# A two-layer block with a mixture of experts: the experts' feed-forward in 4 slabs of 896 columns instead of 7 of 512, and their outputs kept in DRAM

## The chip, the cores and the metric

The kernel runs on one core of one Trainium2 chip. The metric is the device time of one execution in microseconds; the kernel before was timed in three runs. TensorE is written PE, VectorE DVE, ScalarE ACT, GpSimd POOL, and SP is SyncE, which issues the loads of the weights.

## The reference

The input is 256 tokens of 1024 numbers with 16 learned meta tokens ahead of them, all in float32. Each of two layers has a mixer (a pooled branch and differential attention, gated and projected) and a feed-forward. The feed-forward of layer 0 is dense, that of layer 1 is a mixture of 8 experts of which every token uses 2.

```python
def moe_swiglu(h, router, wg, wu, wd):
    logits = jnp.einsum('bld,de->ble', h, router).astype(jnp.float32)
    top_vals, top_idx = lax.top_k(logits, TOP_K)
    top_w = jax.nn.softmax(top_vals, axis=-1)
    combine = jnp.sum(jax.nn.one_hot(top_idx, N_EXPERTS, dtype=jnp.float32) * top_w[..., None], axis=-2)
    out = jnp.zeros_like(h)
    for e in range(N_EXPERTS):
        out = out + combine[..., e:e + 1] * swiglu(h, wg[e], wu[e], wd[e])
    return out
```

`swiglu(h, wg, wu, wd)` is `(silu(h @ wg) * (h @ wu)) @ wd`; `wg` and `wu` are 1024 x 3584 per expert, `wd` is 3584 x 1024. The sum with the residual goes through a last RMS norm.

## The kernel before

**Products in parts.** Every float32 operand is split into a rounded part (float32r, "hi") and the rest ("lo"), and a product is three matmuls: hi with hi, hi with lo, lo with hi. The `Weights` class streams all weights in the order in which they are used. SP loads blocks of 1 MB into raw slots (L87); a block is split in two pieces of 128 x 1024, ACT writing `whi` (L97) and DVE `wlo` (L98) into 5 buffers each. A raw slot comes free, and the next load is issued, behind the second split of its block. `take` keeps four pieces split ahead of the products.

**The stage of the mixture.** Layer 0 and the mixer of layer 1 come first. `MoeNorm` then puts the residual into token order (transposes L800, copy to `h2`), the router's logits are formed (L791), DVE finds the two best experts of a token (L821 to L826), and PE forms each token's rank in its expert (L829, L831, `ppos`). `prepare` builds, for an expert, a 0/1 matrix `s` of tokens and 128 slots (L906), gathers its tokens by matmuls of 128 columns into `pgat` (L916), multiplies them with the norm's gain (L920), splits them into `exh` and `exl` (L921, L922), transposes `s` into `sT` (L926) and forms the slots' scales (L928).

An expert has 7 steps of 512 feed-forward columns. In a step `up` runs twice (gate and up): 24 matmuls of 512 columns (L943 to L945) into one PSUM bank, tokens as the stationary operand. SiLU (ACT, L1047) and the product with up (DVE, L1052) give `gs`; `turn` transposes it by 4 PE transposes (L951) and splits it into `hh` and `hl`. `down` adds the step before into `y`, two banks of 512 columns, 24 matmuls (L991 to L995):

```python
for hf in range(2):
    nc.tensor.matmul(E.y[hf], h[0][:, f], wh[:, 0, d], start=a, stop=False)
    nc.tensor.matmul(E.y[hf], h[1][:, f], wh[:, 0, d], start=False, stop=False)
for hf in range(2):
    nc.tensor.matmul(E.y[hf], h[0][:, f], wl[:, 0, d], start=False, stop=z)
```

At an expert's end `weigh` scales `y` by the expert's weight and splits it (L1003, L1004), and `scatter` (L1010) brings it to token order with 8 matmuls of 512 columns, which accumulate over all experts in four banks `acc`. After the last expert `down_last` finishes one bank of `y` at a time, DVE adds `h2` and `acc` (L1103), and the last norm runs (L1118).

The order on each engine is that of a list scheduler over the program; `high_priority` and `issue_after` move single pieces.

## Time and profile before

| | us |
|---|---|
| runs | 1619.3, 1621.45, 1621.15 (median 1621.15) |
| span of the profiled execution, first to last instruction | 1617.4 |
| time of the profiled execution itself | not listed beside its span |
| PE / DVE / ACT / POOL busy | 1597.8 / 1334.4 / 1093.7 / 4.8 |
| weights loaded by SP's queue | 449.97 MB, 78.7% of 16 engines' span |

The median stands 3.75 us above the profiled span. Times inside the execution are counted from the span's start. The mixture's first up product starts at 611.16 us, its last down product ends where the last scatter starts, at 1603.80. Starts of matmuls that follow each other are compared, not their listed durations, since they overlap on PE.

### The profile page before, as it was taken

How to read it: one execution, taken by the hardware profiler on the slowest of the kernel's cores; microseconds unless marked ns; L12 is line 12 of the kernel's file. 1: busy time of each engine (PE TensorE's matmuls, PEld its weight loads, DVE VectorE, ACT ScalarE, POOL GpSimd, SP SyncE). 2: the span in 40 equal slices, each digit the busy share in tenths (PEclk: the TensorE clock that was granted, in tenths of full speed). 3: DMA queues.
4: the chain of work that ended last, by engine and by line, in shares of the span. 5: the costliest groups of instructions: out<-in, count | busy, mean ns of one | idle time of the engine just before them, and what ended most of it. 6: DMA issues, size and time to landing. Idle time of an engine off the chain costs nothing. (4 is left out here: it accounts for less than half of the span.)

```text
span 1617.4 us, 24251 instructions
## 1 busy us (share of the span) xinstructions
PE 1597.8 (99%) x9315; PEld 1407.3 (87%) x9315; DVE 1334.4 (83%) x1708; ACT 1093.7 (68%) x1349; POOL 4.8 (0%) x12
## 2 busy tenths in 40 slices
PE   8999999999999999999999999999999999999997
PEld 7989999999999998888888888888888888888885
DVE  7857776666877668998899889998999899899897
ACT  5456554444555657777787787778778778778785
POOL 1000000000000000000000000000000000000000
PEclk9999999999999999999999999999999999999998
DMA  9734555555554588999999999999999999999951
GB/s 307 245 113 150 182 172 169 182 173 168 184 160 142 168 331 312 342 364 360 333 365 357 345 358 358 341 362 361 345 354 364 344 349 374 336 346 377 351 205 41
DMA packets 238897, 452.53 MB, mean 280 GB/s; under 512 B 9386, under 2 KB 82264, under 8 KB 238776
## 3 DMA queue, kind: packets, MB, share of 16 engines
q1 hardware_dynamic: 237264, 449.97, 78.7%
q8 instruction: 75, 1.23, 0.3%
q0 software_dynamic: 384, 0.85, 0.2%
q14 instruction: 46, 0.38, 0.1%
q10 hardware_dynamic: 1128, 0.11, 0.1%
HBM read 449.82 MB, written 1.08 MB: 279 GB/s over the span
## 5 line engine op out<-in xcount | busy, mean ns | idle before, releaser
L97 ACT ACTIVATE whi<-raw 128x1024 fp32r<-128x1024 f32 x852 | 892.5, 1060 | 434.9 <-PE ps L386 200.4
L98 DVE TENSOR_TENSOR wlo<-raw,whi 128x1024 fp32r<-128x1024 f32 x852 | 1020.4, 1223 | 153.6 <-ACT whi L97 132.9
L943 PE MATMUL pup<-whi,exh 128*128 128x512 f32 x896 | 354.1, 395 | 0.1
L944 PE MATMUL pup<-wlo,exh 128*128 128x512 f32 x896 | 351.3, 392 | 0.0
L945 PE MATMUL pup<-whi,exl 128*128 128x512 f32 x896 | 349.9, 390 | 0.0
L945 PEld LDWEIGHTS pup<-whi,exl 128*128 128x128 f32 x896 | 168.2, 188 | 34.9
L943 PEld LDWEIGHTS pup<-whi,exh 128*128 128x128 f32 x896 | 168.3, 188 | 33.8 <-DVE exl L922 0.2
L944 PEld LDWEIGHTS pup<-wlo,exh 128*128 128x128 f32 x896 | 168.5, 188 | 33.3
L991 PE MATMUL y<-whi,hh 128*128 128x512 f32 x440 | 175.0, 398 | 0.0
L992 PE MATMUL y<-whi,hl 128*128 128x512 f32 x440 | 174.0, 396 | 0.0
L995 PE MATMUL y<-wlo,hh 128*128 128x512 f32 x440 | 137.7, 394 | 0.0
L386 PE MATMUL ps<-xh,whi 128*128 128x272 f32 (+1 forms) x448 | 131.9, 300 | 0.4 <-ACT hT L707 0.3
L386 PE MATMUL ps<-xh,wlo 128*128 128x272 f32 (+1 forms) x448 | 126.0, 287 | 0.0
L386 PE MATMUL ps<-xl,whi 128*128 128x272 f32 (+1 forms) x448 | 125.9, 286 | 0.0
L386 PE MATMUL ps<-fh,wlo 128*128 128x272 f32 x432 | 124.9, 289 | 0.0
L386 PE MATMUL ps<-fh,whi 128*128 128x272 f32 x432 | 124.8, 290 | 0.0
L386 PE MATMUL ps<-fl,whi 128*128 128x272 f32 x432 | 124.3, 288 | 0.0
L995 PEld LDWEIGHTS y<-wlo,hh 128*128 128x128 f32 x440 | 82.8, 188 | 19.4
L992 PEld LDWEIGHTS y<-whi,hl 128*128 128x128 f32 x440 | 83.0, 189 | 19.1
L991 PEld LDWEIGHTS y<-whi,hh 128*128 128x128 f32 x440 | 82.9, 188 | 18.3
L386 PEld LDWEIGHTS ps<-xh,whi 128*128 128x128 f32 x448 | 84.5, 191 | 4.4 <-PE s L448 1.1
L386 PEld LDWEIGHTS ps<-xl,whi 128*128 128x128 f32 x448 | 83.5, 188 | 0.3
(287 smaller groups left out, 2024.6 us busy)
## 6 DMA issues: line engine op xcount, KB each, us to landing
raw<-in_moe_w_gate_dram SPq DMA_DIRECT2D x112, 1024.0 KB, 5.5
raw<-in_moe_w_up_dram SPq DMA_DIRECT2D x110, 1024.0 KB, 5.7
raw<-in_moe_w_down_dram SPq DMA_DIRECT2D x108, 1024.0 KB, 5.8
raw<-in_w_in_dram SPq DMA_DIRECT2D x30, 1024.0 KB, 6.3
raw<-in_dense_w_gate_dram SPq DMA_DIRECT2D x14, 1024.0 KB, 5.1
raw<-in_dense_w_up_dram SPq DMA_DIRECT2D x14, 1024.0 KB, 5.1
raw<-in_dense_w_down_dram SPq DMA_DIRECT2D x14, 1024.0 KB, 5.0
raw<-in_w_out_dram SPq DMA_DIRECT2D x8, 1024.0 KB, 5.1
```

The costliest lines, as they stand in the source:

```text
L97: self.nc.scalar.activation(hi, w, AF.Copy)
L98: self.nc.vector.tensor_sub(lo, w, hi.bitcast(F32))
L386: newest[0] = nc.tensor.matmul(ps, w_[part][:, k, ms_], xp[:, k, sl], start=t == 0 and k == 0, stop=t == 2 and k == nk - 1).ins
L943: nc.tensor.matmul(ps, E.xh[:, k], wh[:, i], start=k == 0, stop=False)
L944: nc.tensor.matmul(ps, E.xh[:, k], wl[:, i], start=False, stop=False)
L945: nc.tensor.matmul(ps, E.xl[:, k], wh[:, i], start=False, stop=k == NCH - 1)
L991: nc.tensor.matmul(E.y[hf], h[0][:, f], wh[:, 0, d], start=a, stop=False)
L992: nc.tensor.matmul(E.y[hf], h[1][:, f], wh[:, 0, d], start=False, stop=False)
L995: nc.tensor.matmul(E.y[hf], h[0][:, f], wl[:, 0, d], start=False, stop=z)
```

## The change

Everything about layer 0 and the mixer of layer 1 keeps its products. In the mixture:

- **Slabs.** An expert has 4 slabs of 896 columns (`SLAB`), each computed as two halves of 448 columns in two PSUM banks (`SW`). A slab takes 2 x 96 matmuls of 448 columns (L1006), 7 transposes (L1018) and 42 matmuls of 512 columns for `y` (L1044). In the mixture that is 3072 up matmuls of 448 columns in place of 2688 of 512, the same 1344 of `y`, the same 224 transposes in 32 turns in place of 56.
- **Order in a product.** `up` alternates between the two banks in the pattern that `y` has: two matmuls on one bank, two on the other, and for the lo part of the weights one and one.
- **Whole blocks.** A mixture block is 128 x 1792 (gate, up) or 128 x 2048 (down; the last of a slab 128 x 1024), is loaded as one DMA and split by one ACT and one DVE instruction (L115, L116) into 4 hi and 3 lo buffers. Raw slots in the mixture are 13 in place of 16. A row in DRAM is 3.5 KB (896 columns) for gate and up; the block of down takes two neighbouring rows (8 KB) to a partition, so that the columns of `gs` go to the transposes with a stride of 2 (`chunk`).
- **Gain.** The residual is multiplied with the norm's gain on DVE in token order (`h2g`, L843), and `prepare` does not multiply `pgat`.
- **Outputs in DRAM.** `h2` is written to `hdram` (POOL's queue). `keep` scales an expert's `y` on ACT into `yout` and POOL's queue writes it to `ydram`; `weigh` and `scatter` stay for the last expert only, and `sT` is made for it only. In the last expert's slabs 1 and 2, `residual` loads the residual back (`hsum`), gathers each token's rows from `ydram` by four indirect DMAs, and adds them on DVE. Row numbers are formed in `overflow_data`, which also clears one row of `yout` (L950).

```diff
+    def slot(self, i, name):
+        return self.slots[i].tile([P, 2048], F32R, tag=f"w{i}", name=name)
...
+        if large:
+            m = self.n_large
+            self.n_large += 1
+            parts = [self.slot(m % NHI, f"whi{b}"), self.slot(NHI + m % NLO, f"wlo{b}")]
...
+    def add_down(e, s, c0, m):
+        for b in range((NSC + 1) // 2):
+            r = s * SLAB + b * 256
+            n = min(2, NSC - 2 * b)
+            src = moe_w_down[0, e, r:r + n * P, c0:c0 + m]
+            blocks.append((src.rearrange("(p k) f -> p k f", k=n), 1, None))
...
-                nc.scalar.activation(self.h2[:, t, hf * 512:hf * 512 + 512], pt, AF.Copy)
+                d = slice(hf * 512, hf * 512 + 512)
+                nc.vector.tensor_mul(self.h2g[:, t, d], pt, self.gain[:, d])
+                nc.scalar.activation(self.h2[:, t, d], pt, AF.Copy)
                 nc.scalar.activation(pt, pt, AF.Square, accum_out=self.sq[:, t, hf:hf + 1])
+            if hf:
+                nc.gpsimd.dma_start(hdram.rearrange("(t p) d -> p t d", p=P), self.h2)
...
+    def up(E, name, between=None):
+        ps = two(name)
+        for b in range(4):
...
+            wh, wl = ws.take()
+            for w, xs_ in ((wh, (E.xh, E.xl)), (wl, (E.xh,))):
+                for i in range(2):
+                    k = b * 2 + i
+                    for hf in range(2):
+                        f = slice(hf * SW, (hf + 1) * SW)
+                        for x_ in xs_:
+                            nc.tensor.matmul(ps[:, hf, 0:SW], x_[:, k], w[:, i, f], start=k == 0 and x_ is E.xh and w is wh,
+                                             stop=k == NCH - 1 and w is wl)
+        return ps[:, :, 0:SW]
+
+    def chunk(ci):
+
+        b, i = ci // 2, ci % 2
+        return slice(b * 256 + i, (b + 1) * 256, 2) if ci < NSC - 1 else slice(b * 256, SLAB)
+
+    def turn(hs, hh=None, hl=None):
+        pt = two("pth").rearrange("p h (c s) -> p (h c) s", s=P)[:, 0:NSC]
+        for ci in range(NSC):
+            p = nc.tensor.transpose(pt[:, ci], hs[:, chunk(ci)], ident)
...
+    def keep(E, e):
+        nc.scalar.activation(yout, E.y.rearrange("p h d -> p (h d)"), AF.Copy, scale=E.rc[:, 1:2])
+        nc.gpsimd.dma_start(ydram[e * CAP:(e + 1) * CAP], yout)
...
+    def residual():
+
+        pool, tag = ws.kept.pop(0)
+        hsum = pool.tile([P, 2, D], F32, name="hsum", tag=tag)
+        nc.gpsimd.dma_start(hsum, hdram.rearrange("(t p) d -> p t d", p=P))
+        yield hsum
+        spare_row = exl[:, NE % 2].rearrange("p c s -> p (c s)").bitcast(F32)
+        for t in range(2):
+            for k, to in enumerate((yout, spare_row)):
+                nc.gpsimd.indirect_dma_start(out=to, out_offset=None, in_=ydram[:, :],
+                                             in_offset=bass.IndirectOffsetOnAxis(ap=rows_of[:, t, k:k + 1], axis=0),
+                                             bounds_check=None, oob_is_err=True)
+                nc.vector.tensor_add(hsum[:, t], hsum[:, t], to)
+            yield
```

PE, the up product in the steady part of the mixture. `pup` and `pgate` are the PSUM results, `exh` and `exl` the two parts of an expert's tokens, `whi` and `wlo` those of a piece of weights. Before, all on one bank:

```order
L943 MATMUL pup<-whi_1_9410,exh 128x512
L944 MATMUL pup<-wlo_1_9411,exh 128x512
L945 MATMUL pup<-whi_1_9410,exl 128x512
L943 MATMUL pup<-whi_1_9410,exh 128x512
L944 MATMUL pup<-wlo_1_9411,exh 128x512
L945 MATMUL pup<-whi_1_9410,exl 128x512
```

In the changed kernel, behind the end of one slab (`gs` is the product of gate and up, `pth` its transpose):

```order
L1006 MATMUL pup<-wlo_7112,exh 128x448 x4
L1018 MATMUL pth<-cst,gs 128x128 x7
L1006 MATMUL pgate<-whi_7129,exh 128x448
L1006 MATMUL pgate<-whi_7129,exl 128x448
L1006 MATMUL pgate<-whi_7129,exh 128x448
L1006 MATMUL pgate<-whi_7129,exl 128x448
L1006 MATMUL pgate<-whi_7129,exh 128x448
```

The moving rows went from 512 to 448 columns; hi and lo tokens alternate, each pair on one bank, and the lo weights take four matmuls in a row over both banks.

PE, where an expert's output used to be scattered (`acc` are the four banks in token order, `sT` the transposed slot matrix; the `exh` and `exl` that stand in these rows hold the two parts of the weighted output). Before:

```order
L945 MATMUL pup<-whi_1_9410,exl 128x512
L1010 MATMUL acc_7114<-exh,sT 128x512
L1010 MATMUL acc_7116<-exh,sT 128x512
L1010 MATMUL acc_7115<-exh,sT 128x512
L1010 MATMUL acc_7117<-exh,sT 128x512
L1010 MATMUL acc_7114<-exl,sT 128x512
L1010 MATMUL acc_7116<-exl,sT 128x512
L1010 MATMUL acc_7115<-exl,sT 128x512
L1010 MATMUL acc_7117<-exl,sT 128x512
L943 MATMUL pup<-whi_0_9436,exh 128x512
```

In the changed kernel, the end of an expert's down product and of its turn:

```order
L1018 MATMUL pth<-cst,gs 128x128 x3
L1044 MATMUL y<-wlo_8037,hh 128x512 x4
L1044 MATMUL y<-whi_8054,hh 128x512
L1044 MATMUL y<-whi_8054,hl 128x512
L1044 MATMUL y<-whi_8054,hh 128x512
L1044 MATMUL y<-whi_8054,hl 128x512
L1044 MATMUL y<-wlo_8055,hh 128x512 x2
L1018 MATMUL pth<-cst,gs 128x128 x4
L1006 MATMUL pgate<-whi_8072,exh 128x448
L1006 MATMUL pgate<-whi_8072,exl 128x448
L1006 MATMUL pgate<-whi_8072,exh 128x448
```

No scatter stands there; the transposes are placed inside and behind the down product, and the next gate product follows.

DVE, the router's chain at the end of layer 1's mixer (`m` and `i` the best values and their places, `oh` the one-hot experts, `sel` the chosen ones, `pos` the ranks, `s` the slot matrix). Before:

```order
L821 MAX m_7066<-lg_6785 128x8
L821 MAX m_7066<-lg_6786 128x8
L822 MAX_INDEX i_7067<-m_7066,lg_6785 128x8
L822 MAX_INDEX i_7067<-m_7066,lg_6786 128x8
L869 TENSOR_TENSOR wt<-m_7066 128x2
L823 CAST if_7068<-i_7067 128x4
L824 TENSOR_TENSOR oh<-cst,if_7068 128x32
L826 TENSOR_TENSOR sel<-oh 128x16
L889 COPY pack<-sel 128x16
L833 COPY pos<-ppos 128x16
L866 TENSOR_TENSOR rv<-sq_6787 128x2
L906 TENSOR_SCALAR s<-cst,pos,sel 128x128 x2
```

In the changed kernel (`h2g` the residual times gain, `yout` the row that is cleared):

```order
L866 MAX m_6868<-lg_6609 128x8
L866 MAX m_6868<-lg_6610 128x8
L843 TENSOR_TENSOR h2g<-pth_6885,gainb 128x512
L843 TENSOR_TENSOR h2g<-pth_6893,gainb 128x512
L867 MAX_INDEX i_6869<-m_6868,lg_6609 128x8
L867 MAX_INDEX i_6869<-m_6868,lg_6610 128x8
L918 TENSOR_TENSOR wt<-m_6868 128x2
L950 MEMSET yout 1x1024
L868 CAST if_6870<-i_6869 128x4
L869 TENSOR_TENSOR oh<-cst,if_6870 128x32
L915 TENSOR_TENSOR rv<-sq_6611 128x2
L871 TENSOR_TENSOR sel<-oh 128x16
```

Two multiplications of 512 columns and the clearing of the row of 1024 now stand between MAX and `sel`, and the split ahead of MAX is one of 1792 columns in place of 1024.

## Rows read from the trace of the kernel before

**Rows 1.** The page of the profile, busy time of the engines.

```profile
span 1617.4 us, 24251 instructions
PE 1597.8 (99%) x9315; PEld 1407.3 (87%) x9315; DVE 1334.4 (83%) x1708; ACT 1093.7 (68%) x1349; POOL 4.8 (0%) x12
```

**Rows 2.** Windows of stages: us, busy time of each engine, clock, DMA share, GB/s.

```profile
604.00:608.00 4.00, 3.41 (x17) 3.44 (x18) 2.57 (x19) 2.97 (x4) 0.00 (x0) 0.60 1.03 388
640.00:1560.00 920.00, 920.00 (x4254) 759.95 (x4253) 829.63 (x785) 720.71 (x760) 0.00 (x0) 1.00 0.98 354
```

**Rows 3.** Waits of the queue that issues the loads, 700 to 1500 us: total, times, longest.

```profile
SPq L87 <- DVE wlo L98: 666.2, 264, 4.0
```

**Rows 4.** PE timeline: start, duration, instruction; one up product, one bank.

```profile
1567.13 0.39 PE L943 MATMUL pup<-whi,exh 128*128 128x512 f32 x1
...
1575.06 0.40 PE L945 MATMUL pup<-whi,exl 128*128 128x512 f32 x1
```

**Rows 5.** PE timeline: a y product into two banks, then a turn.

```profile
1575.30 0.40 PE L991 MATMUL y<-whi,hh 128*128 128x512 f32 x1
...
1580.18 0.40 PE L992 MATMUL y<-whi,hl 128*128 128x512 f32 x1
1580.41 0.60 PE L951 MATMUL pth<-cst,gs 128*128 128x128 f32 x4
1580.77 0.48 PE L943 MATMUL pup<-whi,exh 128*128 128x512 f32 x1
```

**Rows 6.** PE timeline: the last y product, one bank, to the last scatter.

```profile
1599.70 0.39 PE L1018 MATMUL y<-whi,exh 128*128 128x512 f32 x1
...
1603.80 0.63 PE L1010 MATMUL acc<-exh,sT 128*128 128x512 f32 x2
```

**Rows 7.** PE timeline: products of 256 columns in layer 1.

```profile
593.49 0.28 PE L386 MATMUL ps<-ml,whi 128*128 128x256 f32 x1
...
596.09 0.28 PE L386 MATMUL ps<-mh,wlo 128*128 128x256 f32 x1
```

**Rows 8.** PE timeline: the scatter of one expert.

```profile
1000.74 1.09 PE L1010 MATMUL acc<-exh,sT 128*128 128x512 f32 x4
...
1002.60 0.39 PE L943 MATMUL pup<-whi,exh 128*128 128x512 f32 x1
```

**Rows 9.** PE timeline: a piece of a gather, and the slots' transposes and scales.

```profile
649.41 0.83 PE L916 MATMUL pgat<-s,h 128*128 128x128 f32 x6
650.00 0.48 PE L944 MATMUL pup<-wlo,exh 128*128 128x512 f32 x1
650.31 0.40 PE L945 MATMUL pup<-whi,exl 128*128 128x512 f32 x1
...
686.91 0.38 PE L926 MATMUL pst<-cst,s 128*128 128x128 f32 x2
687.13 0.51 PE L928 MATMUL pst<-rc,s 128*128 128x2 f32 x4
687.49 0.48 PE L944 MATMUL pup<-wlo,exh 128*128 128x512 f32 x1
```

**Rows 10.** PE timeline: router, first gather and the first up product.

```profile
603.14 0.40 PE L829 MATMUL ppos<-sel,cst 128*128 128x16 f32 x2 [1.36 <-DVE sel L826]
604.59 1.01 PE L916 MATMUL pgat<-s,h 128*128 128x128 f32 x4 [0.83 <-DVE s L906]
...
611.16 0.50 PE L943 MATMUL pup<-whi,exh 128*128 128x512 f32 x1
```

**Rows 11.** Groups of instructions, 700 to 1500 us: busy us, mean ns, idle before.

```profile
L98 DVE TENSOR_TENSOR wlo<-raw,whi 128x1024 fp32r<-128x1024 f32 x541 | 644.9, 1223 | 75.5 <-ACT whi L97 62.6
L955 DVE TENSOR_TENSOR hl<-pth,hh 128x512 fp32r<-128x512 f32 x45 | 30.8, 684 | 0.0
L1052 DVE SCALAR_TENSOR_TENSOR gs<-pup,rcs,gs 128x512 f32<-128x512 f32 x45 | 33.6, 746 | 0.0
```

**Rows 12.** A window in which 1 MB blocks stood queued: same columns as Rows 2.

```profile
576.00:584.00 8.00, 8.00 (x71) 8.00 (x70) 3.86 (x8) 2.63 (x4) 0.00 (x0) 1.00 1.04 400
```

More of the change, by code (lines that the diff above doesn't have):

```diff
@@ L101, in split @@
         if i == npc - 1:
-            self.free.append(self.raw.pop(b)[1])
+            slot = self.raw.pop(b)[1]
+            if self.keep:
+                self.keep -= 1
+                self.kept.append(slot)
+            else:
+                self.free.append(slot)
             self.load()
@@ L107, in take @@
         self.taken += 1
-        while self.n_split < min(q + 1 + self.ahead, len(self.order)):
+        large = self.blocks[self.order[q][0]][2] is None
+        ahead = NLO if large else NPAIR
+        while self.n_split < min(q + ahead, len(self.order)):
+            b = self.order[self.n_split][0]
+            if not large and self.blocks[b][2] is None:
+                break
             self.split()
@@ L910, in prepare @@
         E.yparts = []
+        pg_ = two("pgat").rearrange("p h (c s) -> p (h c) s", s=CAP)
         for hf in range(2):
-            pg_ = bank("pgat")
-            for i in range(4):
-                c = hf * 4 + i
+            for c in range(hf * 4, hf * 4 + 4):
                 for t in range(2):
-                    nc.tensor.matmul(pg_[:, i * P:(i + 1) * P], h2[:, t, c * P:(c + 1) * P], E.s[:, t],
-                                     start=t == 0, stop=t == 1)
-            xh_, xl_ = E.xh[:, hf * 4:hf * 4 + 4], E.xl[:, hf * 4:hf * 4 + 4]
@@ L1069, in tile_block, with between @@
-            prev = (E, j, hs)
+                    next(gen)
+                elif s == 2:
+                    for _ in gen:
+                        pass
+            elif s == 1:
+                fin = residual()
+                hsum = next(fin)
+            elif s == 2:
+                for _ in fin:
+                    pass
+            if end:
+                spare_h = [x_[:, NE % 2, 0:NSC] for x_ in (exh, exl)]
+                def between():
+                    with tc.high_priority():
+                        h, ins = turn(gs, *spare_h)
+                    last_h.append(h)
+                    return ins
+                last_h = []
+                down(prev[0], prev[1], turned, between)
+            else:
+                if prev is not None:
+                    down(prev[0], prev[1], turned)
+                    if prev[1] == NS - 1:
+                        keep(prev[0], e - 1)
+                turned, _ = turn(gs)
@@ L1070, in tile_block @@
+            prev = (E, s)
         if e + 1 < NE:
-            for _ in gen:
-                pass
             E = nE
-    free = [slot for slot in ws.free if slot[0] is mn.raw]
+    free = list(ws.free)
     def spare(shape, name):
```

282 lines of the change are left out of this document (137 added, 145 removed).

## Prediction

> **What bounds the kernel now.** Start at the page: PE is busy 1597.8 of the span of 1617.4 us, DVE 1334.4, ACT 1093.7 [rows 1]. Such a share is an average, so the windows come next: from 640 to 1560 us, nearly the whole mixture, PE is busy 920.00 of 920.00 us at the full granted clock, DVE 829.63 and ACT 720.71 [rows 2]. No wait ends on PE there. The DMA share of 0.98 looks like a second bound, and the queue's waits tell that it isn't: SP waited 264 times, 666.2 us in all, for DVE's splits to free a raw slot, so the loads run ahead and stop for room [rows 3]. The mixture is therefore a dense stream of matmuls, and its time is the number of steps times the time from one start to the next. The change is to be costed on PE's timeline.
>
> **The steps.** Sums are made against the profiled span; the median of the runs is 3.75 us above it, and I carry that over. An up product on one bank goes from 1567.13 to 1575.06 in 35 steps, 0.2266 us each [rows 4]. A y product, which changes banks, goes from 1575.30 to 1580.18 in 21 steps, 0.2324 each [rows 5]. The last y product, on one bank with hi and lo in y's order, takes 18 steps in 4.10 us, 0.2278 [rows 6]. The scatter, which changes banks at every step, takes 8 in 1.86, 0.2325 [rows 8]. So a change of bank goes with about 0.005 us more per step of 512 columns. A step of 256 columns takes 2.60/22 = 0.1182 [rows 7]; from there to 0.2266 is 0.423 ns a column, so that 64 columns are worth 0.0271 us.
>
> The mixture's stream lasts from 611.16 [rows 10] to 1603.80 [rows 6], 992.6 us. In it 2688 up steps by 0.2266 are 609.1, 1344 y steps by 0.2324 are 312.3, seven scatters 13.0, 56 turns by 0.36 (1580.41 to 1580.77 [rows 5]) 20.2. That leaves 38.0. Seven gathers of 32 rows, at 0.59 for 6 [rows 9], are 22.0, and seven pieces of slot work by 0.58 [rows 9] are 4.1. The last 11.9 us are longer steps behind interruptions: the first wide step behind a piece of narrow matmuls takes 0.31 [rows 9] in place of 0.23. There are 91 such interruptions (56 turns, 28 gather pieces, 7 of slot work), so 0.13 each.
>
> **Part by part.**
> - *Slabs.* 3072 steps of 448 columns replace 2688 of 512. The changed up has y's pattern of banks and of hi and lo, so I take y's step less 64 columns: 0.2324 - 0.0271 = 0.2053 us. Bounds: 0.1995 if the premium of bank changes vanishes (0.2266 - 0.0271), 0.2054 if all of the scatter's stays. 3072 x 0.2053 = 630.7 against 609.1: **+21.6** (lower end +3.8). The y steps stay 1344 in their old pattern: 0.
> - *Scatter.* Seven of eight go, all on PE's path: **-13.0**. Their transposes of `s` go too, 686.91 to 687.13 [rows 9], 7 x 0.22 = **-1.5**.
> - *Turns.* The 224 transposes stay, in 32 turns. The changed order cuts the wide stream 71 times in place of 91: 20 x 0.13 = **-2.6**. Their stationary reads now have a stride of 2; no row shows such a read. From below, 0; from above, a doubled transpose, 0.09 more for 192 of them, 17 us. I take 0, since a transpose's weights load beside the work of the step ahead and 0.36/4 is well under a wide step.
> - *Router.* PE waited 1.36 us for `sel` and 0.83 for `s` [rows 10], while the granted clock was 0.60 from 604 to 608 [rows 2], a mean of its levels of 1.2 and 2.4 GHz. DVE's order now has between MAX and `sel` two multiplications of 512 columns (0.68 each by `hl`'s row [rows 11]) and the clearing of 1024 elements of one row (an estimate of 0.9, by the slope below): about +2.4, and the first gather behind it. What comes back: no multiplication of `pgat` between gather and split (0.7, once exposed). I take **+2.0**, between 0 and +5.
> - *Splits.* DVE's row for 1024 columns is 1223 ns, for 512 it is 684 [rows 11]: 1.05 ns a column. A split of 1792 is then 2.03 us, of 2048 2.30. A slab has 8 of the first, 3 of the second and one of 1024, 24.4 us; `hl` and `gs` of 896 columns add 1.1 and 1.15. DVE has 26.7 us of work in a slab of 96 x 0.2053 + 42 x 0.2324 + 0.75 = 30.2: hidden, as ACT's lighter load is. If this cover went, each 1% more on DVE's 26.7 beyond 30.2 would show in full.
> - *DRAM traffic.* `keep`, the residual out and back and the gathers add 0.52 x 7 + 1.05 + 1.05 + 2.1 = 7.8 MB to 352 MB of the mixture's weights (8 x 3 x 1024 x 3584 numbers of 4 bytes): 2%. On 354 GB/s [rows 2] that asks for some 362; with blocks queued the engines moved 400 [rows 12]. Hidden. `keep` holds `y`'s banks for one ACT pass of 1024 columns while the next expert's gate and up run for 20 us: hidden. POOL's queue carries all of the new transfers but has none of the weights behind it. The four adds wait for their gathers, and DVE's splits stand behind them; by the changed order they come a slab after the issue. Bounds 0 to 4 x 2; I take 0.
> - *Tail.* The last y product, one scatter, the last norm: unchanged, 0.
>
> Sum: 21.6 - 13.0 - 1.5 - 2.6 + 2.0 = **+6.5**. 1617.4 + 6.5 + 3.75 = **1627.7 us**, 0.4% slower. With the transition's bounds and 0.001 us either way on 3072 steps the case runs from 1620 to 1634. About 0.2%, or 3.2 us, can be told from no change here.
>
> **Rival 1, not slower: narrower steps carry no premium.** If the extra of bank changes hides under the shorter step, up costs 3072 x 0.1995 = 612.9, 17.8 less, and the time is 1609.9. For it: no row shows two banks at under 512 columns. Against it: y and scatter agree on 0.232 with different patterns. It decides from a step of 0.2021 on, where the sum is 9.8 lower and the result under 1618. The Trainium skill, "TensorE: Matmul & The Clock Gate", section "Wait — 56ns, not 53.3ns?", has a rule of this sort: a step is columns over 2.4 GHz plus about 2.5 ns whatever the matmul does, 189 ns here and 216 for 512 columns, so that up would grow by an estimated 1.0 us only and the time be near 1607. The trace disagrees on 512 columns, with 226.6 and 232.4 ns.
>
> **Rival 2: strided transposes.** If their reads double a transpose, +17 gives 1645. It decides from 0.02 us each (3.8 us). For it: nothing shown. Against it: the load of weights overlaps.
>
> **Rival 3: splits become the bound.** If DVE's wide splits cost 16% more than the line through two points, DVE has 24.4 x 1.16 + 2.25 = 30.55 us per slab, and 0.35 over PE's 30.2 in each of 32 slabs gives +11, 1639; it decides from 14% on, and each further 1% costs 8 us. For it: DVE is already at 0.90 of the stage, and there are 3 lo buffers for 5. Against: each buffer is larger, and a split has 2.46 us of PE work to hide under.
>
> **Chances.** Forecast 0.57, rival 1 0.26, rival 2 0.06, rival 3 0.11. The forecast's case falls to slower with 0.38, to the same 0.16, to faster 0.03; rival 1 gives faster 0.24 and same 0.02; the others are slower. Faster 0.27, same 0.18, slower 0.55. The range goes from 1609 (rival 1 in full) to 1638, which leaves out the far ends of rivals 2 and 3 and little of rival 1.
>
> **What to look for.** In the changed profile: starts of up's matmuls 0.205 us apart (0.1995 is rival 1); no scatter until the end; the step from one transpose to the next 0.09 as now; no waits of PE for `wlo` in the mixture; the first up product at 613. PE waiting for splits, or for weights still under way, would make the prediction wrong; so would a stream that starts 5 us late.

## The result and the profile after

The changed kernel takes 1647.89 us (median of 4 runs, 1647.37 to 1649.53) against 1620.22 for the kernel before on the same chip: ratio 1.0169, 95% interval 1.0155 to 1.0184. The forecast was 1627.7 with a range to 1638: the sign was right, the size was not, and the time lies outside the range. Against +6.5 us the profiled span grew by 28.4, from 1617.4 to 1645.8 (the medians by 27.7). The page's first lines answer to [rows 1]:

```profile
span 1645.8 us, 24255 instructions
PE 1607.7 (98%) x9629; PEld 1471.7 (89%) x9629; DVE 1285.4 (78%) x1356; ACT 1017.9 (62%) x996; POOL 15.9 (1%) x27
```

DVE and ACT are less busy than before, by 49 and 76 us; the span is longer all the same. So no engine took over as the bound by its load. The windows (columns as in [rows 2]) tell where the time went. First of the changed kernel, then the two halves of the mixture in the kernel before:

```profile
604.00:608.00 4.00, 0.95 (x4) 0.86 (x4) 2.64 (x15) 3.95 (x9) 1.22 (x2) 0.83 0.86 310
608.00:612.00 4.00, 2.95 (x14) 2.98 (x15) 3.59 (x26) 1.25 (x2) 0.00 (x0) 0.50 0.54 196
640.00:1100.00 460.00, 460.00 (x2285) 410.83 (x2284) 389.20 (x222) 330.14 (x213) 1.61 (x3) 1.00 0.96 353
1100.00:1560.00 460.00, 453.97 (x2213) 397.89 (x2213) 376.29 (x214) 311.50 (x209) 4.84 (x7) 1.00 0.94 354
```

```profile
640.00:1100.00 460.00, 460.00 (x2137) 380.35 (x2136) 414.81 (x395) 359.56 (x380) 0.00 (x0) 1.00 0.98 354
1100.00:1560.00 460.00, 460.00 (x2119) 379.60 (x2118) 414.82 (x391) 361.15 (x381) 0.00 (x0) 1.00 0.98 355
```

Read the counts of PE beside its busy time. Before, the second half has 18 matmuls fewer than the first; after, 72 fewer. These 54 at 460/2285 us each are 10.9 us, while the window shows only 6.0 of idleness, since part of every standstill counts as busy. A step's listed time is 0.36 us where the next one starts 0.20 later, so that the first 0.16 of a wait lies inside the step ahead of it: in the stream the 25 wide steps ahead of a listed wait are longer than their neighbours by 0.16, the 27 behind one by 0.11, and ten steps from 1586 to 1590 us, behind the longest wait, run at a granted clock of 0.57. These are 8.5 us. In the first half PE never stands still. The loss begins in mid-mixture, in a program whose loop does the same in every slab. The waits of PE from 616 to 1612 us name the engines (total, times, longest); the kernel before had no wait of PE at all from 612 to 1600 us:

```profile
PE pgate L1006 <- ACT whi L115: 2.7, 2, 2.6
PE pup L1006 <- ACT whi L115: 2.6, 10, 0.3
PE y L1044 <- DVE wlo L116: 2.3, 3, 0.8
PE pup L1006 <- DVE wlo L116: 1.7, 10, 0.2
PE pth L1018 <- DVE gs L1120: 1.2, 1, 1.2
```

The splits come late, on engines that are busy for 0.7 and 0.83 of the stage. Are the loads late? No: the queue still waits for free slots, 664.0 us in all from 700 to 1500 us against 666.2 before [rows 3]:

```profile
SPq L94 <- DVE wlo L116: 664.0, 303, 6.7
```

ACT's own waits, from 616 to 1612 us, tell what stands in the way:

```profile
ACT hh L1022 <- PE y L1044: 62.8, 13, 9.2
ACT gs L1118 <- PE pgate L1006: 54.0, 19, 5.4
```

Two more of ACT's instructions wait for PE, `exh` (29.7 us, 8 times) and `yout` (17.0, 4 times); no run moved them. DVE's product with up (`gs`) waits as well:

```profile
DVE gs L1120 <- PE pup L1006: 22.0, 9, 3.8
```

Before, ACT's SiLU waited 16.0 us in 54 waits and never over 0.3, and its copy of the turned slots (`hh`) not at all:

```profile
ACT gs L1047 <- PE pup L945: 16.0, 54, 0.3
```

ACT's timeline of the changed kernel shows one slab early and one late in the mixture:

```profile
712.00 1.71 ACT L115 ACTIVATE whi<-raw 128x1792 fp32r<-128x1792 f32 x1 [0.78 <-PE pgate L1006]
713.61 0.99 ACT L1118 ACTIVATE gs<-pgate,rcs 128x896 f32<-128x896 f32 x1
714.50 1.90 ACT L115 ACTIVATE whi<-raw 128x2048 fp32r<-128x2048 f32 x1
...
1203.06 4.87 ACT L115 ACTIVATE whi<-raw 128x1792 fp32r<-128x1792 f32 x3
1211.98 1.01 ACT L1118 ACTIVATE gs<-pgate,rcs 128x896 f32<-128x896 f32 x1 [4.04 <-PE pgate L1006]
1212.88 10.28 ACT L115 ACTIVATE whi<-raw 128x1792 fp32r<-128x1792 f32 x6
```

At 713 us the SiLU follows splits that already stand ahead of PE. At 1212 ACT has nothing to do for 4.04 us: the SiLU is next in its order and waits for the gate product to end, with six splits behind it, which then run without a pause. PE comes to the end of what is split 2.65 us later:

```profile
1214.63 0.47 PE L1006 MATMUL pup<-whi,exh 128*128 128x448 f32 x1 [0.25 <-ACT whi L115]
```

The instruction order of ACT, which is fixed before anything runs, already has this. The first piece is from the third slab, the second from the twentieth; of its three splits ahead of the SiLU two are still the gate product's own:

```
452 L115 ACTIVATE whi_7465<-raw_7201 128x1792
453 L115 ACTIVATE whi_7483<-raw_7219 128x1792
454 L115 ACTIVATE whi_7504<-raw_7237 128x1792
455 L115 ACTIVATE whi_7522<-raw_7258 128x1792
456 L1118 ACTIVATE gs<-pgate,rcs 128x896
...
696 L115 ACTIVATE whi_11413<-raw_11160 128x1792
697 L115 ACTIVATE whi_11431<-raw_11185 128x1792
698 L115 ACTIVATE whi_11449<-raw_11203 128x1792
699 L1118 ACTIVATE gs<-pgate,rcs 128x896
700 L115 ACTIVATE whi_11467<-raw_11221 128x1792
```

Counted through the program, by blocks split ahead of a SiLU beyond those that its own gate has used, it is 4 in the first 13 slabs and then 3, 3, 2, 1, 2, 2, 1, 1 and so on to the end; ahead of `hh` it falls from 4 to 2. Ahead of DVE's product with up it is 2 blocks in the first 15 slabs and then 1 or 0. In the kernel before it is 4 pieces (once 5) and 5 in all 56 steps. That is the first theory to test: **order**, not load. Its rivals are the price of the steps (448 columns, two banks, the stride), the larger blocks, too few buffers, and the DRAM outputs.

The rest of the 28.4 us stands at both ends. Times by landmark of PE (last transpose of layer 1; first of the steady wide stream; first step of the last y product; end of the span):

| us | before | after | diff |
|---|---|---|---|
| to the last transpose of layer 1 | 601.4 | 602.5 | +1.1 |
| transition | 9.8 | 13.6 | +3.8 |
| the stream | 987.1 | 1002.2 | +15.1 |
| last y product to the end | 19.1 | 27.5 | +8.4 |

Transition, PE's timeline (answers to [rows 10]), then DVE's:

```profile
602.48 0.42 PE L841 MATMUL pth<-cst,hT 128*128 128x128 f32 x2
606.56 0.54 PE L874 MATMUL ppos<-sel,cst 128*128 128x16 f32 x2 [3.67 <-DVE sel L871]
609.05 3.75 PE L975 MATMUL pgat<-s,h2g 128*128 128x128 f32 x16 [1.53 <-DVE s L966]
613.55 0.47 PE L1006 MATMUL pgate<-whi,exh 128*128 128x448 f32 x1 [0.75 <-ACT exh L977]
```

```profile
603.09 0.24 DVE L866 MAX8 m<-lg 128x8 f32<-128x8 f32 x2
603.24 1.27 DVE L843 TENSOR_TENSOR h2g<-pth,gainb 128x512 f32<-128x512 f32 x2
605.01 0.91 DVE L950 MEMSET yout<- 1x1024 f32 x1 [0.15 <-issue]
606.34 0.17 DVE L871 TENSOR_TENSOR sel<-oh 128x16 f32<-128x16 f32 x1
```

`h2g` and the clearing of a row stand between the maximum and `sel`, 1.27 and 0.91 us. PE stands still for 3.67 in place of 1.36, and the clock is at its lower level, 1.2 GHz, from 608 to 612.

### The profile page after: what moved, and what is told of

Same layout as the page of the kernel before. It is cut to its first block, busy times and chain, and to the rows that moved or that the text cites. A ratio compares the mean times of both kernels' runs of the same rounds, so it can differ in the third digit from the quotient of the medians.

```text
span 1645.8 us, 24255 instructions
## 1 busy us (share of the span) xinstructions
PE 1607.7 (98%) x9629; PEld 1471.7 (89%) x9629; DVE 1285.4 (78%) x1356; ACT 1017.9 (62%) x996; POOL 15.9 (1%) x27
## 3 DMA queue, kind: packets, MB, share of 16 engines
q0 software_dynamic: 2688, 9.24, 1.5%
## 5 line engine op out<-in xcount | busy, mean ns | idle before, releaser
L116 DVE TENSOR_TENSOR wlo<-raw,whi 128x1792 fp32r<-128x1792 f32 (+2 forms) x388 | 762.6, 2001 | 130.1 <-ACT whi L115 56.0
L115 ACT ACTIVATE whi<-raw 128x1792 fp32r<-128x1792 f32 (+2 forms) x388 | 637.5, 1682 | 143.1 <-PE y L1044 72.8
L115 ACT ACTIVATE w<-raw 128x1024 fp32r<-128x1024 f32 x180 | 189.7, 1058 | 251.3 <-PE ps L418 185.5
L116 DVE TENSOR_TENSOR w<-raw,w 128x1024 fp32r<-128x1024 f32 x180 | 219.3, 1222 | 66.6 <-ACT w L115 66.1
L1006 PE MATMUL pgate<-whi,exh 128*128 128x448 f32 x512 | 189.1, 369 | 3.5 <-ACT whi L115 2.7
L1006 PE MATMUL pup<-whi,exh 128*128 128x448 f32 x512 | 188.2, 368 | 2.6 <-ACT whi L115 2.6
L1006 PE MATMUL pgate<-whi,exl 128*128 128x448 f32 x512 | 187.7, 367 | 0.0
L1006 PE MATMUL pup<-whi,exl 128*128 128x448 f32 x512 | 187.1, 365 | 0.0
L418 PE MATMUL ps<-xh,w 128*128 128x272 f32 (+1 forms) x896 | 177.1, 293 | 0.2 <-ACT hT L739 0.2
L1044 PE MATMUL y<-whi,hh 128*128 128x512 f32 x434 | 171.9, 396 | 0.0
L1044 PE MATMUL y<-whi,hl 128*128 128x512 f32 x434 | 171.7, 396 | 0.0
L418 PE MATMUL ps<-fh,w 128*128 128x272 f32 x864 | 164.5, 290 | 0.0
L1006 PE MATMUL pup<-wlo,exh 128*128 128x448 f32 x512 | 127.5, 371 | 1.7 <-DVE wlo L116 1.7
L1044 PE MATMUL y<-wlo,hh 128*128 128x512 f32 x434 | 123.6, 400 | 2.5 <-DVE wlo L116 2.5
L1006 PE MATMUL pgate<-wlo,exh 128*128 128x448 f32 x512 | 125.8, 368 | 0.2 <-DVE wlo L116 0.2
L1006 PEld LDWEIGHTS pup<-whi,exh 128*128 128x128 f32 x512 | 96.1, 188 | 13.8 <-ACT whi L115 6.3
L1006 PEld LDWEIGHTS pgate<-whi,exh 128*128 128x128 f32 x512 | 96.5, 188 | 12.6 <-ACT whi L115 3.6
L1006 PEld LDWEIGHTS pup<-wlo,exh 128*128 128x128 f32 x512 | 94.0, 188 | 12.5 <-DVE wlo L116 5.5
```

The source lines that it names most:

```text
L115: self.nc.scalar.activation(hi, w, AF.Copy)
L116: self.nc.vector.tensor_sub(lo, w, hi.bitcast(F32))
L418: newest[0] = nc.tensor.matmul(ps, w_[part][:, k, ms_], xp[:, k, sl], start=t == 0 and k == 0, stop=t == 2 and k == nk - 1).ins
L1006: nc.tensor.matmul(ps[:, hf, 0:SW], x_[:, k], w[:, i, f], start=k == 0 and x_ is E.xh and w is wh, stop=k == NCH - 1 and w is wl)
L1044: nc.tensor.matmul(E.y[:, hf], h_[:, ci], w[:, i, d], start=s == 0 and ci == 0 and w is wh and h_ is h[0], stop=s == NS - 1 and ci == NSC ...
```

## The experiments

Ratios are to the kernel before, run on the same chip.

**One bank at a time (x1_bank).** The products of gate and up go through one bank and then the other:

```
-            for w, xs_ in ((wh, (E.xh, E.xl)), (wl, (E.xh,))):
-                for i in range(2):
-                    k = b * 2 + i
-                    for hf in range(2):
+            for hf in range(2):
+                for w, xs_ in ((wh, (E.xh, E.xl)), (wl, (E.xh,))):
+                    for i in range(2):
+                        k = b * 2 + i
```

> The changed kernel, with each block's 12 up matmuls done for one bank and then for the other (2 changes of bank in 12 steps, where there were 8). Its up product takes 9.81 us for 48 steps now, 0.2044 a step. If changes of bank cost, as the forecast had it, a step goes to 0.2007 (the last y product's 0.2278 on one bank less 0.0271) and the time falls by 8 to 12 us, to 1636 to 1640. Rival, that the step of 448 columns is 0.203 whatever the bank: within 2 us of 1648.

Measured: 1637.71 us, ratio 1.0107 (1.0091 to 1.0122), some 10 us below the changed kernel. That lies in the range expected of a cheaper step, but the step is not where the gain comes from. An uninterrupted product of the changed kernel has 24 steps between these two rows, 4.86/24 = 0.2025 us:

```profile
1566.79 0.36 PE L1006 MATMUL pup<-whi,exh 128*128 128x448 f32 x1
...
1571.65 0.39 PE L1044 MATMUL y<-whi,hh 128*128 128x512 f32 x1
1576.32 0.98 PE L1018 MATMUL pth<-cst,gs 128*128 128x128 f32 x7
1577.06 1.17 PE L1044 MATMUL y<-wlo,hh 128*128 128x512 f32 x4
```

In this run, one bank, 24 steps go from 704.16 to 709.02, 0.2025 as well:

```profile
704.16 0.36 PE L1006 MATMUL pgate<-whi,exl 128*128 128x448 f32 x1
...
709.02 0.37 PE L1006 MATMUL pgate<-whi,exl 128*128 128x448 f32 x1
```

The gain is in the stalls, 5.6 us of idle PE in the stream in place of 11.0: the other order of the products gave the scheduler another order on ACT and DVE too. No SiLU has fewer than 2 blocks split ahead of it now, and no product with up fewer than 1.

**No stride (x2_cont).** The slots' transposes read contiguous columns, and the down blocks' DRAM rows are 4 KB again:

```
-        return slice(b * 256 + i, (b + 1) * 256, 2) if ci < NSC - 1 else slice(b * 256, SLAB)
+        return slice(ci * P, (ci + 1) * P)
```

> The changed kernel, with the down blocks loaded so that each chunk of the transposes is 128 neighbouring columns of gs (no stride of 2; DRAM rows of 4 KB in place of 8). Turns take 25.7 us in the changed kernel, 2.3 of it idle, against 19.9 before, for the same 224 transposes. If the stride costs, a transpose goes from 0.105 to 0.090 and the time falls by 3 to 4 us, to 1644 to 1645. Rival, that the longer turns come from seven transposes in a row or from their place in the order: within 1 us of 1648.

Measured: 1648.6, 1.0171 (1.0157 to 1.0185), no difference from the changed kernel. The timeline shows a small price: a turn of 7 takes 0.73 us to the next wide step with the stride (median of the uninterrupted ones), 0.68 without. Over 32 turns that is 1.6 us, well short of the 17 of the rival.

**Buffers, pieces, slabs.** Five runs ask whether room or size holds the splits up. x4_bufs has 5 high and 4 low buffers in place of 4 and 3 and two raw slots fewer:

```
-NRAW, NRAWE, NRAWX, NPAIR, NHI, NLO = 6, 2, 4, 5, 4, 3
+NRAW, NRAWE, NRAWX, NPAIR, NHI, NLO = 6, 2, 2, 5, 5, 4
```

> The changed kernel with 5 hi and 4 lo buffers in place of 4 and 3, and two raw slots fewer. ACT's order still has slabs with only one block of up split ahead of the SiLU. If the number of split buffers is what makes PE wait, stalls of 14 us fall to 2 to 4 and the time to 1636 to 1640; if the order on ACT is, the time stays within 3 us of 1648.

Measured: 1642.76, 1.0137 (1.0120 to 1.0154). Some 5 us better, between the two expectations; the order turns after 11 slabs in place of 13, and PE still stands idle for 9.0 us in the stream.

x5_piece keeps 4 slabs and splits in pieces of 896 and 1024 columns with 7 pairs of buffers:

```
+            blocks.append((src.rearrange("(k p) f -> p k f", p=P), 2, ks(1)))
+            t = self.slot(m % (NHI + NLO), f"w{b}_{i}")
+            parts = [t, t[:, 1024:]]
```

> The changed kernel, with blocks split in pieces of one row group (128 x 896, 128 x 1024), hi and lo side by side in 7 slots, so that PE may start on half a block and splits run 6 pieces (3 blocks) ahead in place of 2 blocks. PE sits idle some 10.6 us between 616 and 1600 in the changed kernel, for whi and wlo. If whole-block splits cause it, idle goes to 0 to 2 and the time falls by 8 to 11 us, to 1637 to 1640. Rival, that ACT and DVE stand behind waits for PE (SiLU, copies of transposes) in any cut: the idle time stays and the time is within 2 us of 1648, or more by the added instructions.

Measured: 1652.63, 1.0192 (1.0177 to 1.0208), a miss: smaller pieces alone do not help. The order turns in this run too, and the transposes now wait for DVE's product (5.6 us in 11 waits).

x3_seven goes back to 7 slabs of 512 in one bank with the matmul order of the kernel before, and keeps the rest, splits of whole 1 MB blocks and DRAM outputs:

```
-NS = 4
-SLAB = DFF // 4
-SW = SLAB // 2
+NS = 7
+SLAB = DFF // 7
+SW = SLAB
```

> The changed kernel with 7 slabs of 512 in one bank, up's order of matmuls as before, blocks of 1 MB split whole (128 x 2048), and the outputs kept in DRAM. If the loss sits in the slabs of 896 (narrow steps +15 to 21, longer last slab +4, part of the stalls), this kernel has before's stream without seven scatters (13.0) and the transposes of s (1.5) and with the later start of the stream (+2 to +5): 1609 to 1614. Rival, that the whole-block splits or the outputs in DRAM cost by themselves: 1625 or more.

Measured: 1626.15, 1.0039 (1.0023 to 1.0054). A miss that taught most: with the steps of the kernel before and 13 us of scatters gone it is still slower than it. x9_seven_piece adds pieces of 1024 by 7 pairs, and x13_five goes to 5 pairs as before (`NPAIR` in place of `NHI + NLO`), after which the stream differs from that of the kernel before by the outputs, the place of the gain, the longer rows of down with their stride, and by whatever order comes out:

> The run with 7 slabs of 512 and outputs in DRAM (1626.15), with its blocks split in pieces of 128 x 1024 as before, in 7 pairs of buffers. That run had before's matmuls less seven scatters (13.0) and the transposes of s (1.5), and yet lost 5.5 us; its stream was 14 us longer than its steps add up to over before's, 8 of it PE waiting for splits. If whole-block splits cause that, the time is 1611 to 1616, under the kernel before; rival, that keeping outputs in DRAM disturbs the stream by itself: 1622 or more.

> The run with 7 slabs of 512, outputs in DRAM and pieces of 128 x 1024 (1638.65), with 5 pairs of split buffers as the kernel before has them, in place of 7. With 7 pairs some 24 us went to steps that follow a late split. If splitting further ahead puts ACT's and DVE's splits in front of what PE's next product needs, the order comes back to before's and the time falls to 1612 to 1620. If DRAM outputs disturb the stream by themselves, it stays at 1630 or more.

Measured: 1638.65, 1.0110 (1.0093 to 1.0126), and 1640.86, 1.0126 (1.0109 to 1.0143). Two more misses, in the same direction: as long as the scheduler sets the order, finer pieces come out worse, and 5 pairs in place of 7 gain nothing. A rival now had to be taken seriously, that the DRAM outputs disturb the stream. But x13_five has its splits 4 and 5 pieces ahead up to about its 28th slab and mostly 2 behind it, and its halves differ as those of the changed kernel do (the windows stand below). Its slabs, pieces and buffers are those of the kernel before, so these sizes alone do not make the order turn.

**The ends.** x7_tail puts the first scatter behind the last down product; x14_trans is x13_five with `h2g` behind `sel` and the clearing of the row two slabs later:

```
-        acc = scatter(E, hf)
+        with tc.issue_after(last_mm[0]):
+            acc = scatter(E, hf)
```

> The changed kernel, with the scatter of the first half of the last expert's output ordered behind the last down product, as the kernel before had it. The part from the start of the last down product to the end takes 27.5 us in the changed kernel and 19.2 before; 4.1 of the 8.4 are 18 more steps of the larger last slab. In it PE waits 1.11 and 0.72 us for the two parts of the output at the first scatter, between the two halves of the last product. If that order is the rest of the loss, the end comes 2 to 3 us earlier, 1645 to 1646; rival, that ACT and DVE are late with splits there anyway: within 1 us of 1648.

```
+                with tc.issue_after(behind) if behind is not None else ExitStack():
+                    nc.vector.tensor_mul(self.h2g[:, t, d], pt, self.gain[:, d])
```

> The run before this one with the router's chain on DVE freed: the two multiplications of h2g ordered behind sel, and the clearing of yout's row moved to the third slab. From the last transposes of layer 1 to the mixture's steady stream takes 13.8 us with 9.8 before. sel comes 3.25 us behind MAX, with 1.05 before. If these two are the later start, this run is 2 to 3 us faster than the run of five pairs; rival, that the clock and the gather in DVE's new order set the start: within 0.7 us of it.

Measured: 1648.29, 1.0168 (1.0151 to 1.0185), and 1640.60, 1.0126 (1.0110 to 1.0143). Neither gained. In x7_tail the waits at the first scatter are gone, but the second half of the last product now waits 2.6 us for DVE's part of the weighing, and the tail grew to 29.5 us. In x14_trans `sel` came earlier, but the first gather then waited 2.1 us for ACT, which reads the same transposes behind `h2g`, and the first wide step 1.8 for ACT's copy: the transition was 15.0 us in place of 13.8.

**The order.** x8_silu puts only SiLU behind the splits emitted ahead of it; x12_order does so for SiLU and `hh` on ACT and for the gated product and `hl` on DVE. Nothing else changes:

```
+        self.last_hi = self.nc.scalar.activation(hi, w, AF.Copy).ins
+        self.last_lo = self.nc.vector.tensor_sub(lo, w, hi.bitcast(F32)).ins
...
+            with tc.issue_after(ws.last_hi):
+                nc.scalar.activation(gs2, pg_, AF.Silu, scale=E.rc[:, 0:1])
...
+        with tc.issue_after(ws.last_hi):
+            a = nc.scalar.activation(hh, pt, AF.Copy)
+        with tc.issue_after(ws.last_lo):
+            v = nc.vector.tensor_sub(hl, pt, hh.bitcast(F32))
```

> The changed kernel, with each SiLU on ACT ordered behind the last split that stands ahead of it in the program. In the changed kernel's order 10 of the last 15 slabs have only one block of up split ahead of the SiLU, which waits up to 5.4 us for the end of gate and holds the splits behind it; here all have two. Stalls and restarts of PE for whi and wlo came to some 14 us, 10 of them in these slabs and 4 at places that stay (the wait at 1581 and three behind turns). If the place of the SiLU causes them, the time falls by 5 to 10 us, to 1638 to 1643. Rival, that two whole blocks ahead are too few in any order, or that loads are late: within 2 us of 1648.

> The changed kernel, with SiLU and the copy of the transposes on ACT, and the product with up and the second copy on DVE, each ordered behind the last split that stands ahead of it in the program. With SiLU alone so ordered, PE's 20 waits for up's splits went, and 13 waits of 0.75 us for y's wlo came in their place, where DVE does the product with up ahead of a split. If the places of these four on two in-order engines are what stalls PE, its waits in the mixture fall from 11 to 0 to 3 us and the time to 1632 to 1637. Rival, that two whole blocks ahead leave too little slack in any order: waits of 8 us or more, and 1643 or more.

Measured: x8_silu 1646.44, 1.0159 (1.0142 to 1.0176), a miss: the time is that of the rival. Still, all waits of `pup` are gone. Stalls stand in `y` instead, for DVE's splits, and DVE now waits longer at its product with up, ahead of which no block is split in 13 of the last 17 slabs (3 in the changed kernel):

```profile
PE y L1044 <- DVE wlo L116: 9.1, 12, 0.8
DVE gs L1121 <- PE pup L1006: 53.6, 19, 3.8
```

x12_order 1635.04, 1.0092 (1.0075 to 1.0108): the time is as expected, and the waits in the stream are 4.4 us, where 0 to 3 were. With all four instructions moved, 12.9 us come back by the medians; in the trace the stream is 12.4 shorter. Only the order differs from the changed kernel, so the order is shown to cost that much. The second half of the mixture, to be compared with 2213 matmuls above, then DVE's and ACT's waits from 616 to 1605 us:

```profile
1100.00:1560.00 460.00, 457.86 (x2249) 405.01 (x2248) 383.14 (x216) 319.65 (x215) 6.75 (x7) 1.00 0.95 358
DVE gs L1124 <- PE pup L1006: 2.4, 5, 0.6
ACT hh L1023 <- PE y L1046: 63.0, 13, 5.9
```

ACT's `hh` waits as long as in the changed kernel. So a wait on a splitting engine is not the loss by itself; what counts is whether enough is split ahead of it, and here at least 2 blocks stand ahead of each of the four in every slab. From x8_silu to x12_order three instructions moved at once; that DVE's product is the one that matters there is read from these waits, and no run moved it alone.

x22_seven_order_only puts the same order on x13_five, x18_seven_order on x14_trans (with both 4 to 5 pieces stand ahead in all 56 steps), and x19_order_bufs joins x12_order with x4_bufs:

> Seven slabs of 512 units and expert outputs in DRAM, pieces of 128x1024 by five buffer pairs, h2g behind sel; new here: every SiLU stands behind four split pieces and every copy of the transposed slots behind four to five in ACT's and DVE's order, as in the kernel before, in all 56 steps. Theory A (the instruction order on the two in-order engines starves TensorE from the middle of the mixture on): the 11 to 14 us of stalls of the run without this order go, the 13 us of scatters stay gone: 1609 to 1615 us, faster than the kernel before. Theory B (the DRAM outputs, by their traffic beside the weights, slow the stream): stalls stay, 1635 to 1642 us.

> The same order of ACT and DVE, but h2g where it was, ahead of sel. Theory A: 1611 to 1617 us, at most 2 to 3 us above the run with h2g moved. Theory B: 1636 to 1643 us.

> The changed kernel (4 slabs of 896) with five buffers of high and four of low weights and three blocks of splits ahead of each SiLU and slot copy in the order. Theory A (look-ahead of the splits in the order decides): 1628 to 1634 us, below the run with the order but two to three blocks (1635). Theory B (two blocks ahead are enough, what is left is larger blocks and 448-column steps): 1634 to 1638 us.

Measured: x22 1620.81, 1.0002 (0.9993 to 1.0011); x18 1623.28, 1.0012 (1.0003 to 1.0021); x19 1635.20, 1.0089 (1.0074 to 1.0104). The order alone is worth 20 us on seven slabs (x13_five to x22; x18, with `h2g` moved too, is no better), and it is not the DRAM outputs, which both kernels have, that cost these 20 us. The windows of x13_five, then of x22:

```profile
640.00:1100.00 460.00, 460.00 (x2125) 380.88 (x2124) 410.06 (x382) 361.71 (x373) 1.61 (x3) 1.00 0.99 361
1100.00:1560.00 460.00, 456.74 (x2052) 366.80 (x2051) 391.29 (x367) 333.95 (x363) 6.26 (x7) 1.00 0.97 355
```

```profile
640.00:1100.00 460.00, 460.00 (x2127) 381.01 (x2126) 409.88 (x381) 361.87 (x373) 1.61 (x3) 1.00 0.98 360
1100.00:1560.00 460.00, 460.00 (x2105) 379.06 (x2104) 408.98 (x378) 360.83 (x376) 5.85 (x7) 1.00 0.99 365
```

The first halves agree to 2 matmuls; in the second, x22 does 53 more. In the whole stream, which is 18.2 us shorter in x22, listed waits fall only from 7.7 to 2.6. But 90 of the up steps of x13_five are longer by 0.11 to 0.20 with no wait listed, 13.1 us in all, against 3.1 in x22: waits short enough to lie inside the listed time of the step ahead. At the first of them behind 1100, DVE's split ends at 1171.08 and the matmul that reads it starts at 1171.13. ACT's waits from 640 to 1560 us, of x13_five and of x22:

```profile
ACT hh L1024 <- PE y L1046: 58.6, 20, 3.6
ACT gs L1120 <- PE pgate L1009: 45.1, 49, 2.7
```

```profile
ACT gs L1123 <- PE pgate L1009: 19.8, 49, 0.5
ACT hh L1025 <- PE pth L1020: 17.8, 22, 0.8
```

x19 has three blocks ahead and hardly a stall, and its stream is 3.8 us shorter than that of x12_order. But its trace loses as much at the ends (layer 1 ends 1.3 later, the transition is 1.1 and the tail 1.5 longer), so that its time is theory B's. For x18 and x22 theory A had the cause and missed the size: they lie 8.3 and 3.8 us above its ranges.

**What is left of those misses.** In x22 the transition takes 16.2 us, and the clock is at 0.50 from 606 to 618. The profiled executions of x22, x23 and x24 took 1623.35, 1622.59 and 1618.85 us, above their medians by 2.5, 2.2 and 1.1, so the transitions read from them may be the longer ones. x23_seven_gain gathers plain tokens and multiplies by the gain behind the gather, as the kernel before does (base: x18); without `h2g` one raw slot also opens earlier. x24_seven_gather also has both halves of the first gather ahead of the first wide step, and frees the first slab's product from the order:

```
+                nc.vector.tensor_mul(pg_[:, cs], pg_[:, cs], moe_gain[:, cs].to_broadcast([P, n, CAP]))
...
+                with tc.issue_after(gathered[0]) if between is not None and k == 0 else ExitStack():
+                    nc.tensor.matmul(ps[:, 0], E.xh[:, k], wh[:, i % 2], start=k == 0, stop=False)
```

> Seven slabs of 512, DRAM outputs and the early order in all steps, as in the run that equalled the kernel before; new: the gather takes the plain tokens and DVE multiplies the gathered block by the gain, as in the kernel before, so that no h2g product stands ahead of the router's choice and no h2g is read by the gather. Theory A (what is left of the 13 us is lost between layer 1 and the mixture: 16.2 us instead of 9.8 to the steady stream, and some 4 us more of wide steps at half clock behind it, because TensorE stands still for 3.9, 1.4 and 0.8 us there): the transition falls to 10 to 12 us and the half-clock steps go: 1609 to 1615 us, faster than the kernel before. Theory B (the gather in one two-bank tile and the tail set it; h2g is beside the path): 1618 to 1622 us.

> The run before with two places changed: both halves of the first expert's gather stand ahead of the first wide step (as in the kernel before; in the last run one half stood behind it), and the first slab's gated product on DVE is no longer held behind the splits (its transposes stalled TensorE for 2.6 us and the clock fell to 0.88 in that stretch). Theory A (TensorE's standstills of 2.1 and 2.6 us and the half clock behind them are the rest): transition 13.7 to 10 to 12 us, the stall at 630 us gone: 1614 to 1618 us, faster than the kernel before by 0.2 to 0.4%. Theory B (the standstill is the wait for ACT's copy of the gathered tokens, which the second half does not cover): 1619 to 1622 us.

Measured: x23 1620.44, 0.9997 (0.9988 to 1.0006), a miss, within theory B: the transition fell to 13.7 us from 15.6 in its base x18, but layer 1 ended 2.4 us later in this trace, and the clock stayed low. The end of layer 1 lies anywhere from 600.6 to 603.8 us in the traces here, so a difference of that size can't be put down to an edit. x24 1617.71, 0.9978 (0.9969 to 0.9988): within the expected range, its transition 11.6 us. **This version beats both kernels**, by 0.2% and 1.8%. It is seven slabs of 512 with the order of the kernel before, and of the change it keeps the expert outputs in DRAM and the longer DMA rows of down, with the stride in the transposes. Of its edits only the transition paid: the stall of the first slab's transposes is still there,

```profile
PE pth L1014 <- DVE gs L1120: 2.6, 1, 2.6
PE pgate L1001 <- ACT exh L974: 1.5, 1, 1.5
```

and between 608 and 620 the granted clock is 0.64, 0.79 and 0.78 in windows of 4 us (before it was back at full from 610 on).

## Why the prediction was wrong, by its own steps

The table takes each instruction of PE's timeline up to the start of the next, less its wait, in the stream.

| term | forecast | shown by the traces |
|---|---|---|
| slabs, 3072 steps | +21.6 | +13.6 (0.2027 a step, median of uninterrupted ones) |
| scatter | -13.0 | -13.1 |
| slot transposes | -1.5 | -1.5 |
| turns: interruptions of the wide steps | -2.6 | -2.4 (99 first steps, longer by 0.083 each, became 68 by 0.085) |
| turns: the transposes | 0 | +3.6 (19.9 to 23.5) |
| router | +2.0 | +3.8, and layer 1 ended 1.1 later |
| stride | 0 | +1.6, contained in the transposes |
| splits | 0 | +11.0 of listed standstill, and 8.5 in the steps beside it |
| gathers | 0 | +0.8 |
| DRAM traffic | 0 | none seen: x22 has it and has no stall in the stream but the first turn's |
| tail | 0 | +8.4, of which 4.1 are steps moved out of the stream |

The first row keeps the forecast's 0.2266 for a step before; the mean of all uninterrupted ones is 0.2276 before and 0.2030 after, which makes it +11.6. With that, the rows of the stream, less the 4.1 moved, come within 1 us of its +15.1.

**The step that failed is "Splits: hidden".** It set DVE's 26.7 us of work against PE's 30.2 in a slab. That sum was right, since DVE is busy for 765 of 920 us, less than in [rows 2]. It shows that the work fits, not that it is done in time. ACT and DVE do their instructions in order, and one that waits for PE's product holds back every split behind it. The forecast costed load and buffers. It asked of the four adds what stands behind them, but not of the SiLU, `hh` and DVE's product with up, though the order of the changed program could have been read before any run. Rival 3 had the right place, PE waiting for splits, by the wrong cause, a DVE that is too slow. x12_order, which adds no capacity, brings back 12.9 us, and the pair x13_five and x22 20. What the runs showed in place of "hidden" is some 19.5 us of PE's time in the stream, 11.0 listed as waits and 8.5 in the steps beside them. Why the scheduler turns from four blocks ahead to one or two in mid-mixture no run here shows.

**Slabs.** The step without its premium, 0.1995, and the step with it, 0.2053, were both wrong: it is 0.2027, and the same on one bank or two. So the premium of the bank change does vanish at 448 columns, as rival 1 had it, but 64 columns fewer give back only 0.0239 us of the 0.2266. The slope through 256 and 512 columns [rows 4, 7] was too steep there. By the rule in the Trainium skill, "TensorE: Matmul & The Clock Gate", section "Wait — 56ns, not 53.3ns?", columns over 2.4 GHz plus about 2.5 ns, this step would take an estimated 189 ns; 202.7 was measured, and the measurement decides. A slab has 2 x 48 up matmuls, 96 as in the sum of the splits, not the 2 x 96 given with the change; 3072 in all is right. With the sum otherwise right this term alone would have made the kernel 1619.7 and no slower, since +6.5 less 8.0 is -1.5: rival 1's time was not reached because of the stalls and the ends.

**Turns.** Fewer interruptions were to save 0.13 each. A first step behind narrow matmuls is longer by 0.08, not 0.13, as the forecast's own 0.31 against 0.23 said; 31 fell away where it counted 20, so the term came out right by two errors. What it put at nothing is the transposes' own time. A turn of 7 takes 0.73 us where 7 transposes by [rows 5] are 0.63; half of the excess is the stride.

**Router and tail.** The bounds 0 to +5 held for the router. For the tail "unchanged" overlooked that the last slab is larger: its last y product has 7 chunks in place of 4, 18 more steps. Between its halves PE now waits for the weighing, which hid under other work before:

```profile
1624.33 0.73 PE L1066 MATMUL acc<-exh,sT 128*128 128x512 f32 x2 [1.11 <-ACT exh L1058]
1625.79 0.74 PE L1066 MATMUL acc<-exl,sT 128*128 128x512 f32 x2 [0.72 <-DVE exl L1059]
...
1632.10 0.74 PE L1066 MATMUL acc<-exh,sT 128*128 128x512 f32 x2 [0.78 <-ACT exh L1058]
```

That is 2.6 us of waiting against 0.63 before (one wait, at 1606.11), so 2.0 of the 4.3 us that remain there. Of the other 2.3, 1.5 pass behind DVE's last row, which ends 6.9 us before the end of the span here and 5.4 in the kernel before.

**The signs to look for.** The first up product came at 613 as forecast (613.55). Two of the signs that were to prove it wrong are there: PE waits for `wlo` from 1120 us on, and the steady stream starts 4.9 us late (616.1 against 611.2).

**What stays open.** x24 sheds 13.1 us of scatters and 1.1 of slot transposes, yet its stream is only 4.6 shorter than that of the kernel before. By the same reckoning, 3.9 of what it loses are in gate and up steps, 1.7 of these at the half clock behind the transition, 2.6 in the stall of the first transposes, 1.9 in the strided turns and 0.6 in the gathers. Its tail is 2.4 us longer. No run took these one by one. x12_order ends 15.7 us above the kernel before in the traces: 9.8 in the tail, 3.8 in the transition and 2.7 in the stream, less 0.7 up to the end of layer 1.

## What to carry to other kernels

Where a stream is bound by one engine and fed by others, an average load under 1 says that the feeders can keep up, not that they do: count, in each feeder's instruction order, how many pieces stand ahead of every instruction that waits for the bound engine, from the first step to the last. A list scheduler's order can turn in mid-program, here even with the slab, piece and buffer sizes of the kernel before; pin it to the emitted order before judging a size. Listed idle time leaves out part of each stall, so compare instructions done in equal windows.

## What the runs showed of the hardware

- A step of 448 columns takes 0.2025 to 0.2027 us on one bank or alternating between two, where 512 columns took 0.2266 on one and 0.2324 on two [rows 4, 5]: what goes with a change of bank disappears with 64 columns fewer.
- Transposes whose stationary operand has a stride of two float32 cost 0.05 us more per turn of 7 than contiguous ones (0.73 against 0.68), 0.007 each.
- A standstill of PE can cost more than itself: in x24 the wait of 1.5 us that ended at 613.07, with the clock low before it, was followed by wide steps of 0.43 us (614.72 to 615.15) until 617.3, nearly twice the 0.2266 of [rows 4]; the granted clock of 612 to 620 us is 0.79 and 0.78. The same is seen behind a standstill in the steady stream: in the changed kernel PE waits 2.59 us until 1585.02, and from 1586 to 1590 us the granted clock is 0.57 and a step takes up to 0.37 us in place of 0.20. Not every one does: in x24 a wait of 2.63 us ended at 629.36, the clock of 620 to 640 is 1.00, and the steps behind the turn are back at 0.23 after one of 0.31.
